# The same kernel with its matmul operands at other SBUF addresses

## The chip, the core and the metric

The kernel runs on one NeuronCore of one Trainium2 chip. The metric is the device time of one execution in microseconds (us); the time before is the median of 3 runs. One execution was also recorded by the hardware profiler; its engines are PE (TensorE matmuls), PEld (TensorE's loads of the stationary operand), DVE (VectorE), ACT (ScalarE), POOL (GpSimd) and SP (which issues most DMAs).

## What is computed

The reference is a network of two blocks on one sequence of 256 tokens with 1024 features, all in float32. The core of it:

```
# first block
h = rms_norm(x);  proj = h @ w_in                      # 1024 x 8352
merged = gate0 * (mla(proj) @ w_br_mla) + gate1 * (dilated(proj) @ w_br_dil) + gate2 * (mem_attention(proj, mem) @ w_br_mem)
x = x + rms_norm(merged @ w_o)
u = rms_norm(x) @ w_ffn_up                             # 1024 x 5632, then a causal convolution of width 3
x = x + rms_norm((silu(gate) * val) @ w_ffn_down)
# second block, two layers
mod = silu(c) @ w_ada + b_ada                          # shift, scale, gate
h = rms_norm(x) * (1 + scale) + shift;  u = h @ w_in_2 # 1024 x 5120
x = x + gate * (concat(rglru(..) * silu(rg_z), mlstm(..) * silu(ml_z)) @ w_out_2)
return rms_norm(x)
```

## The kernel before

Nearly all of the work is matrix products of float32 operands, each written as a sum of two float32r parts. A weight block of 128 partitions and up to 1024 columns comes by DMA into a buffer `raw`; ScalarE casts it to `hi` (L246), VectorE subtracts to get `lo` (L249). Each of `raw`, `hi` and `lo` has four buffers used in turn. The activations are split in the same way: `H` and `L` hold the two parts of the layer's input, eight tiles of 256 tokens in each (8,192 bytes per partition); other pairs, the outputs of attention, the feed-forward's inner activations, the memory's inputs, lie in nine general tiles `s0` to `s8` of the same size ("slots", all shown as `s` in the rows), and the pair of attention outputs in `y`.

Every product is made of three kinds of matmuls (`prod`, L258): activation-high with `hi`, activation-low with `hi`, activation-high with `lo`, four tiles of the contraction at a time. In rows of the trace the name behind the arrow is first the moving operand (the one that streams through the array), then the stationary one (loaded by LDWEIGHTS): `mm<-H,hi` has H moving and the weights stationary, `mm<-hi,s` has the weights moving and a slot stationary. `proj` (features on the partition) streams 256 tokens against 128 weight columns; `proj_long` (token on the partition) streams 512 or 256 weight columns against 128 tokens. There is a load of 128 stationary columns for each matmul, and it runs while the matmul before it streams.

The order of the instructions on each engine is set by the tile framework's scheduler from the program's order and from priorities.

Where a tile lies is set by the order in which the pools are opened, each behind the one before. The lines in question are these:

```
    cp = ctx.enter_context(tc.tile_pool(name="cp", bufs=1))      # constants, xn, H, L
    rawp = ctx.enter_context(tc.tile_pool(name="rawp", bufs=RAW))
    hip = ctx.enter_context(tc.tile_pool(name="hip", bufs=HI))
    lop = ctx.enter_context(tc.tile_pool(name="lop", bufs=LO))
    sp = ctx.enter_context(tc.tile_pool(name="sp", bufs=1))      # slots
...
        hi = hip.tile([P, 1024], F32R, name="hi", tag="hi")
...
        for b in range(0, len(terms), 4):
            for x, y in ((0, 2), (0, 3), (1, 2)):
                for t in terms[b:b + 4]:
                    pe.matmul(dst, lhsT=t[x], rhs=t[y], start=(first and i == 0), stop=(last and i == n - 1))
```

Of the kernel before, what the change touches and what calls it, by code (L numbers as in the profile page):

```python
# [18 lines left out]
P = 128  # L19
S = 256  # L20
# [8 lines left out]
FENCE = 4  # L29
HOLD = 3  # L30
# [77 lines left out]
# products with the token on the partition: output columns in pieces of these widths, as many tiles of rows as make 1024 columns  # L108
# [6 lines left out]
def _long_blocks(kt, pieces=LONG):  # L115
    # for each piece: [(block, tiles)]
    out, n = [], 0
    for w in pieces:
        t = 1024 // w
        out.append([(n + i, range(b, min(kt, b + t))) for i, b in enumerate(range(0, kt, t))])  # L120
        n += len(out[-1])
    return out
# [74 lines left out]
def block_kernel(ctx: ExitStack, tc: tile.TileContext, T: dict, out: bass.AP):  # L197
# [3 lines left out]
    cp = ctx.enter_context(tc.tile_pool(name="cp", bufs=1))  # L201
    rawp = ctx.enter_context(tc.tile_pool(name="rawp", bufs=RAW))
    hip = ctx.enter_context(tc.tile_pool(name="hip", bufs=HI))
    lop = ctx.enter_context(tc.tile_pool(name="lop", bufs=LO))
    sp = ctx.enter_context(tc.tile_pool(name="sp", bufs=1))
# [29 lines left out]
    def hold_loads(*ins):  # L235
        # the next conversions of weights stay behind these instructions of ScalarE and VectorE
        if FENCE:
            fence.update(n=FENCE, ins=[i.ins for i in ins])

    def load(src):  # L240
        n = src.shape[-1]
        raw = rawp.tile([P, 1024], F32, name="raw", tag="raw")[:, :n]
        dma.dma_start(out=raw, in_=src)
        hi = hip.tile([P, 1024], F32R, name="hi", tag="hi")
        with behind(0):
            act.copy(hi[:, :n], raw)  # L246
        lo = lop.tile([P, 1024], F32R, name="lo", tag="lo")
        with behind(1):
            dve.tensor_tensor(out=lo[:, :n], in0=raw, in1=hi[:, :n].bitcast(F32), op=ALU.subtract)  # L249
        fence["n"] -= 1  # L250
        return hi, lo
# [21 lines left out]
    def urgent(on=True):  # L273
        # work at the end of a stage that the tensor engine waits for
        return tc.high_priority(offset=URGENT) if on else nullcontext()

    def proj_long(name, kt, j, H, L, hold=0, beside=(), pieces=LONG):
        # token on the partition, one bank for each block of tokens; the last `hold` weight blocks finish the first tokens early
        w = pieces[j]
        ps = [mm_tile().rearrange("p a b -> p (a b)")[:, :w] for _ in range(2)]  # L280
        blks = _long_blocks(kt, pieces)[j]
        nb = len(blks)
        held = {}

        def part(b, t):
            tb = slice(t * P, (t + 1) * P)
            hi, lo = held[b]
            prod(ps[t], [(H(k)[:, tb], L(k)[:, tb], hi[:, i * w:(i + 1) * w], lo[:, i * w:(i + 1) * w])
                         for i, k in enumerate(blks[b][1])], b == 0, b == nb - 1)

        for b, (n, ks) in enumerate(blks):
            held[b] = load(T[name][n][:, :len(ks) * w])
            if b in beside:
                ada_steps(1)
            if b < nb - hold:
                for t in range(2):
                    part(b, t)
        for t in range(2):
            for b in range(nb - hold, nb):
                part(b, t)  # L300
        return ps

    def proj_first(blks, H, L):
        # tile by tile of the features, one bank for each of the two rows of outputs: starts before all of H is there
        ps = [mm_tile()[:, 0], mm_tile()[:, 0]]
        for k in range(KT):
            hi, lo = (x[:, (k % 4) * 256:(k % 4 + 1) * 256] for x in blks[k // 4])
            for m in range(2):
                mm = slice(m * P, (m + 1) * P)
                prod(ps[m], [(hi[:, mm], lo[:, mm], H(k), L(k))], k == 0, k == KT - 1)  # L310
        return ps
# [17 lines left out]
    ones32 = cp.tile([P, P], F32, name="ones32")  # L329
    dve.memset(ones32, 1.0 / 32.0)  # L330
    eps = cp.tile([P, 1], F32, name="eps")
    dve.memset(eps, EPS)
# [9 lines left out]
    HT = [cp.tile([P, KT, S], F32R, name=n) for n in ("H", "L")]  # L342
# [9 lines left out]
    class Sums:  # L352
        """Sums over the KT tiles of features, token on the partition: one bank for each block of tokens."""
# [5 lines left out]
        def add(self, sq, k):  # L359
            # the first six into the partitions of group k % 4, folded when the last two are still to come  # L360
            if k < 6:
                g = k % 4
                pe.matmul(self.part[32 * g:32 * g + 32], lhsT=ones[:, :32], rhs=sq, start=k < 4, stop=k >= 2)
            if k == 5:
                part = one()
                act.copy(part, self.part)
                self.out = [sm_tile()[:, :P], sm_tile()[:, :P]]
                for t in range(2):
                    pe.matmul(self.out[t], lhsT=part[:, t * P:(t + 1) * P], rhs=ones32, start=True, stop=False)
            if k >= 6:  # L370
                for t in range(2):
                    pe.matmul(self.out[t], lhsT=sq[:, t * P:(t + 1) * P], rhs=ones, start=False, stop=k == 7)
# [9 lines left out]
    def newton(v, n):  # L382
        # 1 / sqrt(v), one Newton step behind the square root
# [8 lines left out]
    def rstd_of(ps, n):  # L392
        # per token, from the sums of squares
# [5 lines left out]
    class Rstd:  # L399
        """1 / sqrt(mean + eps) per token from partial sums of squares, of which the last comes late."""  # L400
# [20 lines left out]
    def root_table(ins):  # L421
        # the square root's table is there before the end of the stage
        with tc.issue_after(ins.ins):
            act.activation(warm, one_c, AF.Sqrt)
# [5 lines left out]
    class Flip:  # L430
        """[token, feature] to [feature, token], four banks of two tiles; a factor per token may go along."""
# [23 lines left out]
    def spread(r):  # L455
        # per-token column to all partitions, token on the free axis
# [50 lines left out]
    def ada_steps(n):  # L507
        # both layers in turn, one step each to finish
# [5 lines left out]
    # =========================== first block ===========================  # L514
    with tc.tile_pool(name="l1", bufs=1) as l1, tc.tile_pool(name="pS", bufs=1) as pS:
# [224 lines left out]
        def dil_proj(p, c, qkv):  # L740
            # queries and keys in turn, then the values
# [65 lines left out]
        # the softmax of a head runs beside the products between its scores and its sums  # L807
# [100 lines left out]
    # the norm's factor is applied to the products of up, before the convolution  # L908
# [36 lines left out]
    # =========================== second block ===========================  # L945
# [10 lines left out]
    def of_head(h, parts):  # L956
        # row 32h on all partitions
# [13 lines left out]
    # half of 8 softplus(-lambda), for both layers  # L971
# [28 lines left out]
    for l in range(2):  # L1000
        # the gate of the layer's output on all partitions, token's side
# [93 lines left out]
        def scores_input(name, h):  # L1095
            # in the place of the memory's input, behind the values
# [56 lines left out]
        em = l2.tile([P, S], F32, name="em", tag="em")  # L1153
# [61 lines left out]
        da = l2.tile([P, S], F32, name="da", tag="da")  # L1215
# [129 lines left out]
```

## Time and profile before

| what | value |
|---|---|
| time, median of 3 runs | 992.81 us (991.2 to 993.47) |
| span of the profiled execution, first to last instruction | 990.5 us |
| what lies between that span and the median | 2.3 us |
| PE busy | 965.9 us (98%), 7,508 matmuls |
| PEld busy | 915.3 us (92%) |
| DVE busy | 736.2 us (74%) |
| ACT busy | 625.1 us (63%) |
| mean granted TensorE clock | 0.994 of full speed |

The profile gives the span of the one execution that it recorded, and no separate time for it; 990.5 us is what the rows of the trace add up to, and the 2.3 us to the median are the start and end of an execution outside them. A matmul's end is modelled in the trace and overlaps the next one's start, so its duration says little; how fast matmuls follow each other is read from their starts.

### The profile page before, as it was taken

The numbers are of one execution on the slowest core, as the hardware profiler recorded it, in microseconds if no ns is written. First come the engines' busy times: TensorE is split into PE (matmuls) and PEld (weight loads), VectorE is DVE, ScalarE is ACT, GpSimd is POOL, SyncE is SP. The second block draws the span as 40 slices with busy tenths as digits, with TensorE's granted clock in tenths as the row PEclk, the third lists the DMA queues.
The fourth block names the chain that finished last, engine by engine and source line by source line (L and its number), as shares of the span: only waits on it lengthen the run. The fifth ranks groups of instructions, "written<-read, shape, count | busy, mean of one in ns | idle before, by whom it ended". The sixth has DMA issues, their size and how long they took to land.

```text
span 990.5 us, 18853 instructions
## 1 busy us (share of the span) xinstructions
PE 965.9 (98%) x7508; PEld 915.3 (92%) x7508; DVE 736.2 (74%) x1267; ACT 625.1 (63%) x1025; POOL 49.9 (5%) x55
## 2 busy tenths in 40 slices
PE   7999999999999999999999999999999999999996
PEld 5999999899989989999979899898989998999986
DVE  5856766667576788888875898588975887687754
ACT  7666555454345478787744786895645876976543
POOL 0000000000000001212200000000002000000021
PEclk9999999999999999999999999999999999999998
DMA  8664575767786746665687365345786355335652
GB/s 295 198 182 136 173 232 193 250 227 225 247 266 211 247 157 206 189 194 190 198 276 244 105 199 168 115 153 194 250 276 200 131 171 170 101 113 193 187 163 75
DMA packets 53225, 190.71 MB, mean 193 GB/s; under 512 B 6064, under 2 KB 6448, under 8 KB 53136
## 3 DMA queue, kind: packets, MB, share of 16 engines
q1 hardware_dynamic: 52128, 185.17, 57.9%
q0 software_dynamic: 1008, 4.33, 1.3%
q8 instruction: 59, 0.97, 0.4%
q14 instruction: 30, 0.25, 0.1%
HBM read 188.42 MB, written 1.05 MB: 191 GB/s over the span
## 4 chain that ended last, share of the span: by engine, by line
PE 71%; DVE 11%; ACT 8%; DMA 6%; issue 4%; POOL 0%; SPq 0%; DVEq 0%; ACTq 0%; POOLq 0%
PE mm L258 59%; DVE lo L249 5%; DMA raw<-in_w_ada 4%; ACT hi L246 3%; ACT fz L934 2%; ACT fw L935 2%; DVE fu L928 1%; PE sm L258 1%; PE sm L1040 1%; DVE raw L494 1%; ACT s L481 1%; PE sm L1196 1%; DMA raw<-in_w_o 1%; PE sm L658 1%; PE sm L1245 1%
## 5 line engine op out<-in xcount | busy, mean ns | idle before, releaser
L249 DVE TENSOR_TENSOR lo<-raw,hi 128x1024 fp32r<-128x1024 f32 (+2 forms) x299 | 372.1, 1255 | 110.4 <-ACT hi L246 108.3
L246 ACT CAST hi<-raw 128x1024 fp32r<-128x1024 f32 (+2 forms) x299 | 308.6, 1042 | 181.2 <-PE mm L258 107.4
L258 PE MATMUL mm<-H,hi 128*128 128x256 f32 x1456 | 238.6, 281 | 0.1
L258 PE MATMUL mm<-L,hi 128*128 128x256 f32 x1456 | 235.8, 279 | 0.1
L258 PE MATMUL mm<-H,lo 128*128 128x256 f32 x1456 | 235.0, 279 | 0.2 <-DVE lo L249 0.2
L258 PEld LDWEIGHTS mm<-H,hi 128*128 128x128 f32 x1456 | 198.9, 188 | 2.2 <-issue 1.6
L258 PEld LDWEIGHTS mm<-L,hi 128*128 128x128 f32 x1456 | 199.0, 188 | 0.4 <-DVE L L1018 0.3
L258 PEld LDWEIGHTS mm<-H,lo 128*128 128x128 f32 x1456 | 198.6, 188 | 0.4 <-DVE lo L249 0.4
L258 PE MATMUL mm<-hi,s 128*128 128x256 f32 (+1 forms) x784 | 149.5, 324 | 0.0
L258 PEld LDWEIGHTS mm<-hi,s 128*128 128x128 f32 x784 | 119.0, 191 | 11.5
L494 DVE CUSTOM_DVE_ANT_0 raw<-raw,c_act 128x1024 f32<-128x1024 f32 x48 | 58.7, 1223 | 55.1 <-DMA raw<-in_w_ada 55.1
L258 PE MATMUL mm<-lo,s 128*128 128x256 f32 (+1 forms) x392 | 85.8, 325 | 2.4 <-DVE lo L249 2.4
L258 PEld LDWEIGHTS mm<-lo,s 128*128 128x128 f32 x392 | 61.7, 192 | 8.8 <-DVE lo L249 3.1
L258 PE MATMUL mm<-s,hi 128*128 128x256 f32 x320 | 56.0, 294 | 0.0
L258 PEld LDWEIGHTS mm<-s,hi 128*128 128x128 f32 x320 | 46.2, 195 | 6.3 <-issue 2.9
L258 PE MATMUL mm<-s,lo 128*128 128x256 f32 x160 | 35.5, 289 | 0.0
L428 ACT ACTIVATE sq<-xn 128x512 f32<-128x512 f32 (+1 forms) x24 | 13.5, 562 | 33.1 <-POOL xn L1309 21.5
L937 POOL TENSOR_TENSOR fz<-fz,fw 128x508 f32<-128x508 f32 x22 | 24.7, 1123 | 130.3 <-DVE fz L936 130.3
L934 ACT ACTIVATE fz<-fu,cols 128x256 f32<-128x256 f32 x44 | 26.1, 594 | 6.5 <-DVE fu L928 6.5
L258 PEld LDWEIGHTS mm<-s,lo 128*128 128x128 f32 x160 | 26.4, 195 | 2.0 <-issue 1.2
L646 ACT ACTIVATE sx<-sx,nm 128x256 f32<-128x256 f32 (+3 forms) x24 | 13.3, 555 | 23.5 <-DVE nm L643 23.5
L481 ACT CAST s<-two 128x512 fp32r<-128x512 f32 x24 | 14.9, 619 | 18.9 <-DVE two L1250 18.9
(315 smaller groups left out, 1146.4 us busy)
## 6 DMA issues: line engine op xcount, KB each, us to landing
raw<-in_w_ada SPq DMA_DIRECT2D x48, 512.0 KB, 4.5
raw<-in_w_up SPq DMA_DIRECT2D x44, 512.0 KB, 4.3
raw<-in_w_out SPq DMA_DIRECT2D x32, 512.0 KB, 4.3
raw<-in_w_down SPq DMA_DIRECT2D x21, 512.0 KB, 4.2
raw<-in_w_mlx SPq DMA_DIRECT2D x16, 512.0 KB, 4.4
raw<-in_w_rgx SPq DMA_DIRECT2D x16, 512.0 KB, 4.2
raw<-in_w_mlo SPq DMA_DIRECT2D x16, 512.0 KB, 4.1
raw<-in_w_rgz SPq DMA_DIRECT2D x16, 512.0 KB, 4.4
```

Of the source, the lines that this page charges most:

```text
L246: act.copy(hi[:, :n], raw)
L249: dve.tensor_tensor(out=lo[:, :n], in0=raw, in1=hi[:, :n].bitcast(F32), op=ALU.subtract)
L258: pe.matmul(dst, lhsT=t[x], rhs=t[y], start=(first and i == 0), stop=(last and i == n - 1))
L428: return act.activation(sq[:, :src.shape[-1]], src, AF.Square, accum_out=acc)
L481: act.copy(hi, src)
L494: dve.tensor_tensor_reduce(out=raw, in0=raw, in1=c_act, op0=ALU.mult, op1=ALU.add, scale=1.0, scalar=0.0, accum_out=mod[:, l, m:m + 1])
L646: act.activation(sx[:, a:b], src, AF.Exp, bias=nm[:, i:i + 1], accum_out=den[:, i:i + 1])
L658: pe.transpose(ps[:, i * P:(i + 1) * P], sx[:, o:o + P], ident)
L928: dve.tensor_tensor(out=u, in0=ps, in1=rs.unsqueeze(1).to_broadcast([P, 2, S]), op=ALU.mult)
L934: act.activation(z[:, i], u[:, i], AF.Identity, scale=col("conv_w", 88 + c), bias=col("conv_b", c))
L935: act.activation(w[:, i], u[:, i], AF.Identity, scale=col("conv_w", c))
L937: pool.tensor_tensor(out=z[:, :, 2:], in0=z[:, :, 2:], in1=w[:, :, :S - 2], op=ALU.add)
```

## The change

The change lays tiles at other addresses. The pool of `H` and `L` now comes first, behind `ones32`, which is widened so that H begins at a multiple of 512 bytes. Then come the pools of `hi` and of `lo`, whose tiles are widened from 1,024 to 1,056 elements (only 1,024 are used), so that each buffer begins 128 bytes further, modulo 512, than the one before. `raw` and the other constants follow, then `eps` as a filler of 32 bytes, then the slots. To make room, the tile `em` takes the buffer of `B`, and `da` that of `R`, in the second block. The comments of the file were taken out too.

```
+STEP = 1056
+FILL_H, FILL_S = 224, 8
...
-    cp = ctx.enter_context(tc.tile_pool(name="cp", bufs=1))
-    rawp = ctx.enter_context(tc.tile_pool(name="rawp", bufs=RAW))
+    hp = ctx.enter_context(tc.tile_pool(name="hp", bufs=1))
+    ones32 = hp.tile([P, FILL_H], F32, name="ones32")[:, :P]
+    dve.memset(ones32, 1.0 / 32.0)
+    HT = [hp.tile([P, KT, S], F32R, name=n) for n in ("H", "L")]
     hip = ctx.enter_context(tc.tile_pool(name="hip", bufs=HI))
     lop = ctx.enter_context(tc.tile_pool(name="lop", bufs=LO))
+    rawp = ctx.enter_context(tc.tile_pool(name="rawp", bufs=RAW))
+    cp = ctx.enter_context(tc.tile_pool(name="cp", bufs=1))
+    fill = ctx.enter_context(tc.tile_pool(name="fill", bufs=1))
+    eps = fill.tile([P, FILL_S], F32, name="eps")[:, 0:1]
+    dve.memset(eps, EPS)
...
-        hi = hip.tile([P, 1024], F32R, name="hi", tag="hi")
+        hi = hip.tile([P, STEP], F32R, name="hi", tag="hi")[:, :1024]
-        lo = lop.tile([P, 1024], F32R, name="lo", tag="lo")
+        lo = lop.tile([P, STEP], F32R, name="lo", tag="lo")[:, :1024]
...
-        em = l2.tile([P, S], F32, name="em", tag="em")
+        em = l2.tile([P, S], F32, name="em", tag="B")
-        da = l2.tile([P, S], F32, name="da", tag="da")
+        da = l2.tile([P, S], F32, name="da", tag="R")
```

The addresses in the two built programs, in bytes from the start of a partition, with the remainder modulo 512 in brackets:

| tile | before | after |
|---|---|---|
| H, L | 33312 (32), 41504 (32) | 17408 (0), 25600 (0) |
| hi, four buffers | 66272, 70368, 74464, 78560 (all 224) | 33792 (0), 38016 (128), 42240 (256), 46464 (384) |
| lo, four buffers | 82656, 86752, 90848, 94944 (all 224) | 50688 (0), 54912 (128), 59136 (256), 63360 (384) |
| raw, four buffers | from 49888 (all 224) | from 67584 (all 0) |
| slots s0 to s8 | from 99040 (all 224) | from 100448 (all 96) |
| y | 196128 (32) | 197536 (416) |

A slice of H, L, a slot or y for one tile of the contraction begins a multiple of 1,024 bytes further on, and one of a weight buffer a multiple of 512, so all slices of a tile have the tile's remainder.

The order of instructions is the same on every engine but for two memsets that VectorE does before anything else. VectorE's first rows before the change (`s_85` and the like are slots; `ones_89` is `ones32`):

```order
L327 MEMSET ones_s 128x256
L330 MEMSET ones_89 128x128
L332 MEMSET eps 128x1
L335 MEMSET one_c 128x1
L477 SCALAR_TENSOR_TENSOR s_112<-s_85,g_mem,s_111 128x256 x2
```

and with it:

```order
L206 MEMSET ones_58 128x128
L214 MEMSET eps 128x1
L337 MEMSET ones_s 128x256
L341 MEMSET one_c 128x1
L482 SCALAR_TENSOR_TENSOR s_118<-s_97,g_mem,s_117 128x256 x2
```

`ones32` and `eps` are set first and `ones_s` behind them; nothing else moved. As an example of the matmuls, a stretch of PE in a product of the first block's gates and the branch product behind it, before (the numbers are those of the tiles):

```order
L258 MATMUL mm_3631<-H_100,hi_3627 128x256 x4
L258 MATMUL mm_3631<-L_101,hi_3627 128x256 x4
L258 MATMUL mm_3631<-H_100,lo_3629 128x256 x4
L258 MATMUL mm_3688<-y_110,hi_3684 128x256 x8
L258 MATMUL mm_3688<-y_110,lo_3686 128x256 x4
```

and with the change, where all numbers are other but the sequence is the same:

```order
L268 MATMUL mm_3637<-H_60,hi_3633 128x256 x4
L268 MATMUL mm_3637<-L_61,hi_3633 128x256 x4
L268 MATMUL mm_3637<-H_60,lo_3635 128x256 x4
L268 MATMUL mm_3694<-y_116,hi_3690 128x256 x8
L268 MATMUL mm_3694<-y_116,lo_3692 128x256 x4
```

Nothing moved there but the lines of the source.

## Rows read from the trace of the kernel before

**Rows 1.** The page: busy time of each engine, granted clock in 40 slices.

```profile
PE 965.9 (98%) x7508; PEld 915.3 (92%) x7508; DVE 736.2 (74%) x1267; ACT 625.1 (63%) x1025; POOL 49.9 (5%) x55
...
PEclk9999999999999999999999999999999999999998
```

**Rows 2.** The page: chain of work that ended last, shares of the span.

```profile
PE 71%; DVE 11%; ACT 8%; DMA 6%; issue 4%; POOL 0%; SPq 0%; DVEq 0%; ACTq 0%; POOLq 0%
```

**Rows 3.** Waits over the whole span: us in total, times, longest.

```profile
DVE lo L249 <- ACT hi L246: 108.3, 113, 4.0
ACT hi L246 <- PE mm L258: 107.4, 100, 3.5
```

**Rows 4.** Groups of matmuls by shape: busy us, mean ns | idle before.

```profile
L258 PE MATMUL mm<-H,hi 128*128 128x256 f32 x1456 | 238.6, 281 | 0.1
...
L258 PE MATMUL mm<-hi,s 128*128 128x512 f32 x288 | 79.6, 395 | 0.0
L258 PE MATMUL mm<-hi,s 128*128 128x256 f32 x496 | 70.6, 283 | 0.0
L258 PE MATMUL mm<-s,hi 128*128 128x256 f32 x320 | 56.0, 294 | 0.0
L258 PE MATMUL mm<-lo,s 128*128 128x512 f32 x144 | 45.6, 397 | 2.4 <-DVE lo L249 2.4
L258 PE MATMUL mm<-lo,s 128*128 128x256 f32 x248 | 40.2, 283 | 0.0
L258 PE MATMUL mm<-s,lo 128*128 128x256 f32 x160 | 35.5, 289 | 0.0
```

**Rows 5.** Timeline of PE, 38 to 73 us: start, us, instruction, count.

```profile
38.42 0.64 PE L258 MATMUL mm<-H,hi 128*128 128x256 f32 x4
...
72.34 0.83 PE L379 MATMUL sm<-ones_s,s 128*128 128x128 f32 x6
```

**Rows 6.** Timeline of PE in the feed-forward's first product, 424 to 478 us.

```profile
424.02 0.62 PE L258 MATMUL mm<-L,hi 128*128 128x256 f32 x4
...
477.51 0.62 PE L258 MATMUL mm<-H,lo 128*128 128x256 f32 x4
```

**Rows 7.** Timeline of PE, 534 to 549 us: weights moving, slots stationary, 256 columns.

```profile
534.12 0.64 PE L258 MATMUL mm<-lo,s 128*128 128x256 f32 x4
...
549.24 0.40 PE L258 MATMUL mm<-hi,s 128*128 128x256 f32 x2
```

**Rows 8.** Timeline of PE: 512 weight columns moving against H and L.

```profile
280.04 0.63 PE L258 MATMUL mm<-hi,L 128*128 128x512 f32 x2
...
282.84 0.63 PE L258 MATMUL mm<-hi,L 128*128 128x512 f32 x2
```

**Rows 9.** Timeline of PE: 512 weight columns moving against slots.

```profile
952.09 0.61 PE L258 MATMUL mm<-lo,s 128*128 128x512 f32 x2
...
958.89 0.61 PE L258 MATMUL mm<-lo,s 128*128 128x512 f32 x2
```

**Rows 10.** Timeline of PE, 315.8 us: float32 matmuls of 128 columns.

```profile
315.83 0.83 PE L783 MATMUL sm<-pt,s 128*128 128x128 f32 x6
316.50 1.50 PE L785 MATMUL sm<-pt,s 128*128 128x128 f32 x12
```

**Rows 11.** Window 380 to 478 us: PE, PEld, DVE, ACT, POOL busy, PEclk, DMA share, GB/s.

```profile
380.00:478.00 98.00, 98.00 (x867) 98.00 (x867) 87.47 (x125) 79.82 (x143) 18.84 (x18) 1.00 0.61 192
```

**Rows 12.** Groups of VectorE by shape: the weights' subtraction, and one half as wide.

```profile
L249 DVE TENSOR_TENSOR lo<-raw,hi 128x1024 fp32r<-128x1024 f32 x293 | 366.9, 1263 | 106.6 <-ACT hi L246 104.5 <-PE mm L258 1.3
...
L482 DVE TENSOR_TENSOR s<-two,s 128x512 fp32r<-128x512 f32 x24 | 16.4, 684 | 4.3 <-ACT s L481 4.1
```

**Rows 13.** Timeline at the start: VectorE's memset of `ones32`, PE's first matmul.

```profile
1.18 0.17 DVE L330 MEMSET ones<- 128x128 f32 x1
...
6.99 1.06 PE L363 MATMUL sm<-sq,ones_s 128*32 128x256 f32 x2 [6.99 <-DVE s L477]
```

More of the change, by code (lines that the diff above doesn't have):

```diff
@@ L328, in block_kernel @@
     ones = ones_s[:, :P]
[L329 to L332, printed above, removed]
     c_act = cp.tile([P, D], F32, name="c_act")
@@ L340, in block_kernel @@
     half = cp.tile([P, 56], F32, name="half")
-    HT = [cp.tile([P, KT, S], F32R, name=n) for n in ("H", "L")]
     H, L = kth(HT[0]), kth(HT[1])
```

## The prediction

> **What bounds the kernel now.** [...] The chain that ended last goes through PE for 71% of the span; the rest is mostly VectorE, ScalarE and DMA, the making of weight blocks [rows 2]. The waits tell how these hang together: VectorE's `lo` waits for ScalarE's `hi` (108.3 us in all), and `hi` waits for matmuls (107.4 us), that is for a buffer that TensorE gives back [rows 3]. The loads are held up by TensorE, not the other way round: what makes matmuls follow each other faster moves nearly everything behind them.
>
> So the distance from one matmul's start to the next is the number to read, by kind of operands. [...]
>
> - H or L moving (address 32 modulo 512), weights stationary (224): from 38.42 to 72.34 us there are 288 matmuls without a break, 33.92 us / 288 = 117.8 ns [rows 5].
> - The same operands at the same addresses in the product of up: 424.02 to 477.51 us, 118 groups of four, 53.49 / 472 = 113.3 ns [rows 6].
> - Weights moving, slots stationary (both 224): 534.12 to 549.24 us, 126 matmuls, 15.12 / 126 = 120.0 ns [rows 7].
> [...]
>
> [...] And one pair of addresses has two steady distances, 117.8 and 113.3; each holds for tens of microseconds. [...]
>
> **The change, part by part.** No instruction is added, and no product, wait or DMA is moved. Three small things first. The two memsets that come earlier are VectorE's, 0.17 us for `ones32`, 5.8 us ahead of TensorE's first matmul, which waits for later things [rows 13]: nothing, and if that cover were gone, 0.2 us. `em` in the buffer of `B` waits for the last reader of `B`, a VectorE addition from whose result `em` is made anyway, and `da` in that of `R` comes after the readers of `R` by a whole stage: nothing. Operands of VectorE and ScalarE move too. The subtraction takes 1,263 ns for 1,024 columns, and one of 512 takes 684 [rows 12], so 579 ns for the second half, 1.13 ns a column, with all three operands at one remainder; I take no change. Were it a tenth dearer, it would be hidden, since VectorE is busy for 736 us of the span [rows 1]; only in the product of up, where it is busy for 87.47 of 98 us [rows 11], would the window's 18 products with 2 subtractions each (36 x 0.126 = 4.5 us) come near the edge.
>
> What remains is TensorE's distance. Modulo 512, moving less stationary was 320 for H and L, and 0 for slots. With the change it depends on the buffer: 0, 384, 256, 128 for H and L, one after the other as the buffers come round; 96, 480, 352, 224 for slots that move, and the opposite of these for slots that stand still. Of these the trace shows only 0, and only with both at 224. So the price has to be bounded. The lower end for 256 columns is 111.7 ns: float32 matmuls with an ordinary load of 128 columns each start 0.67 us / 6 apart [rows 10], the shortest that rows show beside such a load. [...]
>
> Counts [rows 4]: 3 x 1,456 = 4,368 matmuls with H or L moving. Some 1,050 of them are the product of up at 113.3 (22 products of 48; 867 lie in the window of rows 11, 98 us); for the other 3,318 I take 117.8. With slots and 256 columns 496 + 248 + 320 + 160 = 1,224, at 120.0; with 512 columns 288 + 144 = 432, at 226.7.
>
> My choice between the ends: I take it that runs whose loads come from another remainder with each block do not keep to the dearer of two steady states, and 113.3 is a state that these very matmuls hold through all of up. So H and L go to 113.3: 3,318 x 4.5 ns = 14.9 us. Slots leave the distance 0, which is the dearest seen at 256 columns; I take the 117.8 that is next to it: 1,224 x 2.2 = 2.7 us. The 512-column ones I leave where they are. Sum 17.6 us. Of this, between 71% (TensorE's share of the chain) and 97.5% (its busy share) arrives at the end, 12.5 to 17.2 us; I take 90%, 15.8 us, since the loads wait for TensorE. The profiled span goes from 990.5 to 974.7, and with the 2.3 us between span and median the time goes from 992.8 to **977.0 us**.
>
> **The rivals.**
>
> *Nothing changes.* [...] For it: the same addresses give 113.3 and 117.8 [rows 5, 6]. Against it: no stretch of slots reads as H and L do [rows 7], and 512 columns are dearer against H and L than against slots [rows 8, 9]. Time: 992.8, give or take the 4.7 us that up would lose if it fell into the other state (1,050 x 4.5 ns). Chance 0.10. [...]
>
> *Slower: multiples of 128 are as bad as 0.* Distance 0 gave 120.0 ns without exception [rows 7], and H at 0 against the first of the four buffers at 0 is a distance of 0. If what matters repeats every 128 bytes, all of H's and L's matmuls go to 120.0, and up loses its 113.3: 3,318 x 2.2 + 1,050 x 6.7 = 7.3 + 7.0 = 14.3 us, 1,007 us. The point from which it decides is the mean of H and L now, (3,318 x 117.8 + 1,050 x 113.3) / 4,368 = 116.7 ns: above that after the change, the kernel is slower. For it: that buffer, and that 113.3 was reached with an odd multiple of 64. Against it: nothing shows a period of 128. Chance 0.27, milder cases included; at the upper end of the price, 126.7 ns, it would be 29.5 + 14.1 + 8.2 = 52 us (1,045), which I hold for unlikely.
>
> *Half of it.* The buffer at 0 costs 120.0, the other three give 113.3, mean 115.0: 4,368 x 1.7 = 7.4 us, with the slots' 2.7 and the 90% 9.1 us: 983.7. Chance 0.15.
>
> *More than forecast.* [...] Chance 0.13.
>
> **How the numbers follow.** The forecast has 0.35. Faster by over 0.2% (about what a measurement of this kernel can tell from no change) are the forecast, half and more: 0.63. The same is the first rival: 0.10. Slower: 0.27. For eight in ten I leave out the lowest part of the last rival and the upper half of the slower one: 957 to 1,004 us. Within the forecast alone the range is 968 to 982: slots at 120.0 and the share of 71% (14.9 x 0.71 = 10.6 us) to slots at 111.7 and 97.5% ((14.9 + 10.2) x 0.975 = 24.5 us).
>
> **What would show it.** In the profile after, PE's timeline: 33.92 us for the 288 matmuls of rows 5 become 32.6 if H and L go to 113.3, and up keeps its 113.3. Were they apart by buffer, groups of four with `hi` and `lo` of one block would read otherwise than those of the next. Slots: 126 matmuls in 14.8 us, not 15.12. Waits of `hi` for matmuls [rows 3] shrink, and PE's busy share stays near 97%. The prediction is wrong if up is slower than 113.3, if slots go above 120.0, or if PE becomes faster and then waits for `lo`, which would say that the loads are the bound.

## The result, and the profile after

The changed kernel is slower: 997.51 us median of 4 runs (996.38 to 998.86), against 992.53 us of the kernel before on the same chip (991.2 to 993.47, 4 runs). The ratio is 1.0054, with a 95% interval of 1.0039 to 1.0068. The prediction said 977.0 us. The profiled execution has a span of 996.1 us, 5.6 more than before.

The page of the kernel after: busy time of each engine, granted clock in 40 slices, and the chain that ended last. They answer to [rows 1] and [rows 2].

```profile
PE 974.3 (98%) x7508; PEld 922.0 (93%) x7508; DVE 728.0 (73%) x1267; ACT 628.1 (63%) x1025; POOL 50.1 (5%) x55
...
PEclk9999999999999999999999999999999999999999
...
PE 90%; DMA 4%; DVE 3%; ACT 2%; issue 1%; SPq 0%; DVEq 0%; ACTq 0%
```

TensorE is busy for 8.4 us more with the same 7,508 instructions, at a mean granted clock of 0.996 (0.994 before), and it stands in 90% of the chain, where it stood in 71%. So the matmuls follow each other more slowly. Its timeline in the kernel after shows where: first H and L moving, then slots against 256 columns, then slots against 512 columns.

```profile
38.13 0.64 PE L268 MATMUL mm<-H,hi 128*128 128x256 f32 x4
...
72.37 2.39 PE L384 MATMUL sm<-ones_s,s 128*128 128x128 f32 x20
...
522.58 0.63 PE L268 MATMUL mm<-lo,s 128*128 128x256 f32 x4
...
532.49 0.63 PE L268 MATMUL mm<-lo,s 128*128 128x256 f32 x4
...
956.30 0.63 PE L268 MATMUL mm<-lo,s 128*128 128x512 f32 x2
...
963.31 0.63 PE L268 MATMUL mm<-lo,s 128*128 128x512 f32 x2
```

The 288 matmuls of [rows 5] take 34.24 us, 118.9 ns each, where 117.8 stood before and 113.3 was forecast. The slots of [rows 7] improve: 84 matmuls in 9.91 us, 118.0 ns instead of 120.0. The 512 columns of [rows 9], which the prediction left alone, get dearer: 30 in 7.01 us, 233.7 ns instead of 226.7. The product of up is next, in windows of the kernel after (all its matmuls between its first full block and the first of the next product, w_down; then w_down's 130 matmuls of 512 columns). The columns are those of [rows 11].

```profile
369.21:491.30 122.09, 122.09 (x1029) 122.09 (x1028) 95.23 (x149) 99.44 (x172) 22.94 (x21) 1.00 0.59 190
491.30:521.63 30.33, 30.33 (x132) 24.42 (x131) 23.60 (x53) 15.78 (x24) 3.56 (x4) 1.00 0.78 257
```

The same two windows in the kernel before:

```profile
367.01:483.41 116.40, 116.40 (x1030) 116.40 (x1028) 102.46 (x147) 95.29 (x169) 21.72 (x20) 1.00 0.62 194
483.41:517.35 33.94, 31.57 (x132) 25.39 (x131) 26.22 (x56) 18.37 (x28) 4.64 (x5) 0.95 0.76 253
```

Up holds 1,027 matmuls between these two starts, so its distance went from 113.3 to 118.9 ns, and that cost 5.7 us. The next window gives 3.6 us back, although its 512 columns are dearer: TensorE has no gap in it any more (30.33 of 30.33 us busy, 31.57 of 33.94 before) and its granted clock reads 1.00 (before 0.95). What stood there before is this: two rows of TensorE's timeline in the kernel before, and a window of the same kernel just behind them (us, PE busy, granted clock, DMA share, GB/s):

```profile
506.23 1.09 PE L258 MATMUL mm<-hi,s 128*128 128x512 f32 x4
509.70 0.73 PE L258 MATMUL mm<-lo,s 128*128 128x512 f32 x2 [2.37 <-DVE lo L249]
```

```profile
510.00:514.60 4.60, 4.60 (x14) 0.63 0.88 295
```

A 2.37 us wait for VectorE's `lo`, and behind it 4.6 us in which the granted clock reads 0.63 in the mean, 0.50 from 511.1 to 514.5 us. The page's row of 40 slices [rows 1] shows a 9 there. The starts of the windows give the account of the span: the kernel after is 2.2 us late at up (369.21 against 367.01), 7.9 late at w_down (491.30 against 483.41), 4.3 late at its 256 columns (521.63 against 517.35), and 5.6 at the end.

The waits of the loads, in the kernel after, answer to [rows 3]. Both grew, where the prediction had the second shrinking: a buffer comes free later when TensorE is slower.

```profile
DVE lo L259 <- ACT hi L256: 126.8, 116, 4.1
ACT hi L256 <- PE mm L268: 121.4, 122, 3.5
```

### The profile page after: what moved, and what is told of

Its sections match the earlier page's. It is cut to its first block, busy times and chain, and to the rows that moved or that the text cites. A ratio compares the mean times of both kernels' runs of the same rounds, so it can differ in the third digit from the quotient of the medians.

```text
span 996.1 us, 18853 instructions
## 1 busy us (share of the span) xinstructions
PE 974.3 (98%) x7508; PEld 922.0 (93%) x7508; DVE 728.0 (73%) x1267; ACT 628.1 (63%) x1025; POOL 50.1 (5%) x55
## 4 chain that ended last, share of the span: by engine, by line
PE 90%; DMA 4%; DVE 3%; ACT 2%; issue 1%; SPq 0%; DVEq 0%; ACTq 0%
PE mm L268 78%; DMA raw<-in_w_ada 2%; PE sm L268 1%; PE sm L1045 1%; DVE lo L259 1%; DMA raw<-in_w_dv 1%; PE sm L663 1%; PE sm L1201 1%; PE sm L1250 1%; PE sm L790 1%; PE sm L1241 0%; PE sm L724 0%; PE sm L451 0%; DVE raw L499 0%; DMA s<-in_memT 0%
## 5 line engine op out<-in xcount | busy, mean ns | idle before, releaser
L259 DVE TENSOR_TENSOR lo<-raw,hi 128x1024 fp32r<-128x1024 f32 (+2 forms) x299 | 363.8, 1226 | 128.2 <-ACT hi L256 126.8
L256 ACT CAST hi<-raw 128x1024 fp32r<-128x1024 f32 (+2 forms) x299 | 309.3, 1044 | 201.6 <-PE mm L268 121.4
L268 PE MATMUL mm<-H,hi 128*128 128x256 f32 x1456 | 241.3, 284 | 0.1
L268 PE MATMUL mm<-H,lo 128*128 128x256 f32 x1456 | 240.2, 283 | 0.0
L268 PE MATMUL mm<-L,hi 128*128 128x256 f32 x1456 | 238.9, 282 | 0.1
L268 PEld LDWEIGHTS mm<-L,hi 128*128 128x128 f32 x1456 | 202.8, 189 | 0.4 <-DVE L L1023 0.3
L268 PEld LDWEIGHTS mm<-H,lo 128*128 128x128 f32 x1456 | 202.9, 190 | 0.0
L268 PEld LDWEIGHTS mm<-hi,s 128*128 128x128 f32 x784 | 117.4, 189 | 12.9
L486 ACT CAST s<-two 128x512 fp32r<-128x512 f32 x24 | 14.9, 620 | 19.2 <-DVE two L1255 19.2
L268 PE MATMUL mm<-y,hi 128*128 128x256 f32 x192 | 26.7, 281 | 0.0
```

The costliest lines, as they stand in the source:

```text
L486: act.copy(hi, src)
```

## The experiments

**The theories.** The word distance has two meanings here: with ns, the time from one matmul's start to the next; without, the difference of addresses in bytes, moving less next stationary, modulo 512 where nothing else is said. *D*: what counts is the distance between the moving operand and the next stationary one, modulo some power of two. *A*: each operand's own alignment counts. *S*: the remainder that changes from buffer to buffer is what costs. Later ones are stated with the runs.

The table gathers all runs. The distances in ns are means over matmuls that follow each other without a gap; for each matmul the time to the next start was taken from the trace, and its operands' addresses from the program. "Up" is the product of up, "H, L" all others with H or L moving. The times are medians, the ratios to the kernel before on the same chip. The distances come from one profiled execution of each kernel, and it need not be a typical one: e1's was the slowest of ten (994.40 us), e8's the fastest of six (985.83; the slowest took 991.68). In which state runs of matmuls stood in the other executions is not recorded.

```
kernel                 H, L   up     weights  slots on  512 on  us      ratio (95%)
                                     on slots weights   slots
before                 117.7  113.3  119.9    119.6     227.5   992.53
after                  118.9  118.9  118.1    119.2     233.4   997.51  1.0054 (1.0039-1.0068)
e1 old distances       117.4  117.8  119.9    119.5     227.4   991.67  0.9995 (0.9983-1.0007)
e2 H at 64             114.6  113.5  118.1    119.1     233.2   983.48  0.9909 (0.9894-0.9924)
e3 no step             119.8  120.0  118.4    119.6     234.1   1002.18 1.0102 (1.0083-1.0121)
e4 distance 32         116.8  116.7  120.0    119.5     227.3   989.79  0.9973 (0.9959-0.9987)
e5 all at 64           114.4  113.5  116.1    115.3     230.9   978.98  0.9868 (0.9839-0.9896)
e6 64, no step         114.5  113.3  117.6    114.3     229.2   981.48  0.9887 (0.9858-0.9916)
e7 64, step 256        115.2  113.4  115.8    117.6     233.3   984.09  0.9910 (0.9885-0.9936)
e8 64, other half      117.6  113.3  114.4    115.0     229.0   987.97  0.9963 (0.9940-0.9986)
e9 hi and lo apart     114.0  113.3  117.8    116.9     230.0   978.95  0.9861 (0.9841-0.9880)
e10 the same and step  114.1  113.4  117.2    115.4     230.6   979.68  0.9862 (0.9839-0.9885)
```

**e1, the old distances in the new layout.** All pools stand in the new order, but the operands are as far apart modulo 512 as before (H and L 0, all weights and slots 192).

```diff
-STEP = 1056
-FILL_H, FILL_S = 224, 8
+STEP = 1024
+FILL_H, FILL_S = 224, 112
     HT = [hp.tile([P, KT, S], F32R, name=n) for n in ("H", "L")]
+    dve.memset(hp.tile([P, 48], F32, name="pad_h"), 0.0)
```

> The changed layout, but with every distance (moving less stationary, modulo 512) as it was before: H and L at 0, all weight buffers at 192, slots at 192, y at 0. Theory D (the distance decides): H and L against weights go back from 118.9 to 117.8 ns with the product of up at 113.3 or 117.8, slots at 256 columns from 118.4 to 120.0, 512 columns against slots from 233 to 226.7; the time to 992.5 us, or 997 if up falls into its other state. Theory A (each operand's own alignment decides, H at a multiple of 512 being dear): H and L stay at 118.9, 997 us or more. Theory S (the remainder that changes from one weight buffer to the next is what costs): as D, since there is no step.

The timeline of TensorE in this run has the same 288 matmuls in 33.92 us, to the hundredth as before.

```profile
37.73 0.64 PE L269 MATMUL mm<-H,hi 128*128 128x256 f32 x4
...
71.65 2.40 PE L385 MATMUL sm<-ones_s,s 128*128 128x128 f32 x20
```

With other alignments for every operand, the distances and the time (0.9995) are those of before: D holds, A falls, and the rest of the change (order of pools, early memsets, shared buffers) costs nothing outside the interval, which ends at 1.0007. Up fell into its other state here, 117.8 ns, which makes it 4.6 us longer (120.95 against 116.40). Of that, w_down's first window gave back 2.0 (31.90 against 33.94) and a few runs of H and L that started at 113.3 gave 0.8; the profiled span is 2.2 us longer than before, a difference that the medians don't show.

**e2, H and L moved by 64 bytes.** All else is as in the change: weights at 0, 128, 256, 384 and slots at 96.

```diff
-FILL_H, FILL_S = 224, 8
+FILL_H, FILL_S = 240, 8
     HT = [hp.tile([P, KT, S], F32R, name=n) for n in ("H", "L")]
+    dve.memset(hp.tile([P, 112], F32, name="pad_h"), 0.0)
```

> The changed kernel with H and L at 64 modulo 512 instead of 0; the weight buffers keep their steps of 128 (0, 128, 256, 384), slots stay at 96. The distances of H and L are then 64, 448, 320, 192 in turn, all 64 away from a multiple of 128, as before the change. Theory D with a period of 128 or 256: H and L at 117.8 ns in spite of the steps (3,318 x 1.1 = 3.6 us less than the changed kernel), and up at 113.3 if it finds that state again (5.9 us less): 988 to 994 us. Theory S: 118.9 everywhere, 997.5 us. Theory A: no forecast for 64; 997.5 if 64 is as dear as 0.

The timeline of the 288 matmuls again:

```profile
38.93 0.64 PE L269 MATMUL mm<-H,hi 128*128 128x256 f32 x4
39.40 0.63 PE L269 MATMUL mm<-L,hi 128*128 128x256 f32 x4
39.87 0.63 PE L269 MATMUL mm<-H,lo 128*128 128x256 f32 x4
40.34 0.62 PE L269 MATMUL mm<-H,hi 128*128 128x256 f32 x4
40.79 0.62 PE L269 MATMUL mm<-L,hi 128*128 128x256 f32 x4
...
71.62 2.39 PE L385 MATMUL sm<-ones_s,s 128*128 128x128 f32 x20
```

The first three groups of four start 0.47 us apart, the following 0.45: the run enters at 117.8 ns, drops when the buffer changes, and stays there (288 in 32.69 us, 113.5 ns). Not every run drops at its first change of buffer; of that more under e9. The time is 983.48 us, 14.0 less than with the change, for 64 bytes of one pair of operands. S falls: a step between buffers is no cost in itself.

**e3, no step.** Only `STEP = 1024` instead of 1056, so that all weights are at 0, as H and L.

> The changed kernel without the step: all weight buffers at 0 modulo 512, H and L at 0, slots at 96. Distances are then 0 for H and L throughout, 96 for slots that move, 416 for slots that stand. Theory D: H and L at the 120.0 ns that slots at distance 0 had before, 4,368 x 1.1 = 4.8 us more than the changed kernel, 1,002 us; 512 columns stay near 233 ns. Theory S: without the step H and L fall back to 117.8 or less, 994 us or less.

```profile
37.64 0.63 PE L268 MATMUL mm<-H,hi 128*128 128x256 f32 x4
...
72.18 2.40 PE L384 MATMUL sm<-ones_s,s 128*128 128x128 f32 x20
```

That timeline gives 34.54 us / 288 = 119.9 ns. Distance 0 is as dear for H and L as for slots. The 120.0 ns that the rival "multiples of 128 are as bad as 0" had put on all of H and L come true only here, with every buffer at 0, at 1,002 us.

**e4, distance 32 in the old layout.** Eight floats behind H and L in the kernel before bring the distance from 320 to 288; slots stay at 0.

```diff
     HT = [cp.tile([P, KT, S], F32R, name=n) for n in ("H", "L")]
+    dve.memset(cp.tile([P, 8], F32, name="pad_h"), 0.0)
```

> The kernel before with one pad of 32 bytes between L and the weights, which shifts everything behind it by 32: H and L stay at 32, weights, slots at 256. Only the distance of H and L changes, from 320 to 288 (32 modulo 256); slots stay at distance 0 and y at 320. Theory D: in the changed kernel, matmuls at distances 32 and 288 followed each other every 116.7 ns, so H and L go to 116.7 everywhere: 3,318 x 1.1 = 3.6 us less, and up, which had 113.3, 3.6 us more: 992.5 us, no change in the sum, with up at 116.7. Theory A: H has not moved, so up keeps 113.3 and the others 117.8 unless the weights' own alignment (a multiple of 256 instead of 224) counts.

H and L go to 116.8 and up to 116.7, about the figure that `y` shows at 32 and 288 in the kernel after (116.7 to 116.8). That is faster than before (0.9973), although up is 3.4 us longer (119.82 against 116.40); why that costs nothing is told below. The gain lies ahead of up, which starts 2.8 us earlier than before (364.24 against 367.01): 1,374 matmuls with H or L moving take 0.9 ns less each, and from 360.9 to 364.3 us the granted clock reads 1.00 here and 0.50 in the kernel before.

**e5, every pair at an odd multiple of 64.** As the change, with H and L at 0, weights at 64, 192, 320, 448, slots at 256 and y at 128.

```diff
-FILL_H, FILL_S = 224, 8
+FILL_H, FILL_S = 224, 32
     HT = [hp.tile([P, KT, S], F32R, name=n) for n in ("H", "L")]
+    dve.memset(hp.tile([P, 16], F32, name="pad_h"), 0.0)
...
+        dve.memset(l1.tile([P, 16], F32, name="pad_y"), 0.0)
         yT = l1.tile([P, 8, S], F32R, name="y", tag="y")
```

> Every pair of operands an odd multiple of 64 bytes apart (H and L at 0, weight buffers at 64, 192, 320 and 448, slots at 256, y at 128 modulo 512), buffers 128 bytes apart modulo 512 as in the change. Theory K (at such a distance matmuls of 256 columns have two steady pitches, 117.8 and 113.3 ns, and a change of the distance by 128 pushes a run into the shorter): H and L as with H at 64 (114.5 outside up, 113.4 in up), and slots and y now too, from 118.6 to about 114.5 in 1,224 matmuls, 5.0 us; 512 columns half at 228.8 and half at 233, 1 us less; of these 6 us nine tenths arrive: 978 us against 983.5 with H at 64 alone. Rival (the runs of slots are too short, or too mixed, to be pushed): slots stay at 117.8, 982 us. If the making of weight blocks has become the bound by now, pitches fall but the time stays at 983 and the waits of PE for lo grow.

Measured 978.98 us, as K said; slots improve less evenly. The timeline of weights against slots has 12 matmuls from row to row:

```profile
518.06 0.63 PE L269 MATMUL mm<-lo,s 128*128 128x256 f32 x4
...
519.47 0.62 PE L269 MATMUL mm<-lo,s 128*128 128x256 f32 x4
...
520.83 0.62 PE L269 MATMUL mm<-lo,s 128*128 128x256 f32 x4
...
522.20 0.63 PE L269 MATMUL mm<-lo,s 128*128 128x256 f32 x4
...
523.60 0.62 PE L269 MATMUL mm<-lo,s 128*128 128x256 f32 x4
```

1.41, 1.36, 1.37 and 1.40 us: in this direction the runs drop and climb again with the buffers (117.8 and 117.4 at 64 and 320, 113.8 and 115.4 at 192 and 448), while H and L, once at 113.3, stay.

**e6, the same without the step**: e5 with `STEP = 1024`, so all weights at 64.

> The same, but all four weight buffers at 64 modulo 512, so that the distance stays one and the same within a run. Theory K: runs stay in the state in which they began, mostly 117.8, now and then 113.3; H and L 117.5, slots and y 117.8 instead of 119.5 to 120.0 at distance 0, 512 columns near 229: 989 to 990 us. Rival F (an odd multiple of 64 is enough, and the old layout met 117.8 for another reason): H and L at 113 to 114.5, 978 us, as with the step.

```profile
38.34 0.63 PE L269 MATMUL mm<-H,hi 128*128 128x256 f32 x4
...
71.00 2.39 PE L385 MATMUL sm<-ones_s,s 128*128 128x128 f32 x20
...
536.03 0.63 PE L269 MATMUL mm<-lo,s 128*128 128x256 f32 x4
...
538.86 0.63 PE L269 MATMUL mm<-lo,s 128*128 128x256 f32 x4
```

K fails here: 288 matmuls in 32.66 us (113.4 ns) and 114.5 over all H and L, without any change of remainder, 981.48 us. But rival F, which fits H and L, doesn't fit slots: 24 matmuls in 2.83 us, 117.9 ns. H and L stand at 448 (192 modulo 256), where e1 and before had 320 (64 modulo 256).

**e7, buffers 256 bytes apart**: H and L at 128, weights at 192, 448, 192, 448, slots at 256, y at 64.

```diff
-STEP = 1056
-FILL_H, FILL_S = 224, 8
+STEP = 1088
+FILL_H, FILL_S = 128, 1
     HT = [hp.tile([P, KT, S], F32R, name=n) for n in ("H", "L")]
+    dve.memset(hp.tile([P, 16], F32, name="pad_h"), 0.0)
...
-    one_c = cp.tile([P, 1], F32, name="one_c")
-    dve.memset(one_c, 1.0)
+    one_c = ones_s[:, 0:1]
```

> The same again, but the four weight buffers 256 bytes apart modulo 512 (192, 448, 192, 448), H and L at 128, slots at 256, y at 64. The distance changes from block to block, but only by 256. If what matters repeats every 256 bytes, as the pitches by distance in the kernel after say (equal at 0 and 256, at 128 and 384, at 96 and 352), this is no change, and runs stay where they began: 989 to 991 us, H and L at 117.5. Rival (any change of remainder pushes a run): 978 to 980 us, H and L at 114.5.

H and L read 115.2 ns and 984.09 us came out, between K's range and the rival's. Run by run there are only two values, 117.8 and 113.3, and past its first block no run of H and L goes from one to the other: a step of 256 is no step, as K said. Of its 54 runs of H and L 35 settle in the shorter state in their first block, far more than K allowed; that goes with the distance, 192 modulo 256, as in e6, where 42 of 54 do.

**e8, the other half**: e6 with 48 floats behind H and L instead of 16, so that H and L stand at 320 to the weights, and not at 448.

> All four weight buffers at 192 modulo 512, H and L at 0, slots at 384, y at 256: one distance per pair of operands as in the run without a step, but each in the other half of 256 bytes (H and L against weights 320, that is 64 modulo 256, where it was 448, that is 192; slots against weights 192, weights against slots 320, so these two stay in their halves; y 64). Theory B (at odd multiples of 64 there are two steady pitches; a run takes one in its first matmuls and holds it; 192 modulo 256 takes 113.3 mostly, 64 takes 117.8 mostly): H and L go from 114.5 to 117.5 and up from 113.3 perhaps to 117.8, 10 to 15 us, so 991 to 996 us. Rival P (which state a run takes hangs on what runs ahead of it, and not on the half): H and L stay near 114.5, 981 us.

```profile
37.00 0.63 PE L269 MATMUL mm<-H,hi 128*128 128x256 f32 x4
...
70.92 2.39 PE L385 MATMUL sm<-ones_s,s 128*128 128x128 f32 x20
...
533.24 0.62 PE L269 MATMUL mm<-lo,s 128*128 128x256 f32 x4
...
535.96 0.62 PE L269 MATMUL mm<-lo,s 128*128 128x256 f32 x4
```

For H and L, B holds and P falls: the 288 matmuls are back at 33.92 us, and the mean at 117.6. 51 of the 54 runs of H and L settle at 117.8. The time, 987.97 us, is 6.5 above e6, less than expected: in the profiled execution up stayed at 113.3, and weights on slots improved by 3 ns. The slots are what B can't explain: weights on slots at 320 hold 113.3 ns (24 in 2.72 us) where the same distance held 117.9 in e6. So the half of the 256 bytes is not all that picks the state.

**e9, hi and lo 128 bytes apart**: e6 with 32 floats between the pools of `hi` and `lo`; the distance changes inside each block. Slots and `y`, which lie behind, move by 128 bytes with `lo`.

```diff
     hip = ctx.enter_context(tc.tile_pool(name="hip", bufs=HI))
+    mid = ctx.enter_context(tc.tile_pool(name="mid", bufs=1))
+    dve.memset(mid.tile([P, 32], F32, name="pad_m"), 0.0)
     lop = ctx.enter_context(tc.tile_pool(name="lop", bufs=LO))
```

> All hi buffers at 64, all lo buffers at 192, H and L at 0, slots at 384, y at 256: the distance changes by 128 inside each block, from the products of hi to those of lo, and not from buffer to buffer. If a change by 128 pushes a run of H and L into 113.3 and a change back doesn't lift it, every run of H and L reaches 113.3 within its first 12 matmuls: 113.5 everywhere, against 114.35 with the step from buffer to buffer, 3 to 4 us off 979: 975 us. Rival (the push needs a change of buffer, or lasts only as long as the distance 192): H and L between 113.3 and 117.8, 115 to 116, 983 us.

One run of H and L in its timeline, a group of four to a row:

```profile
908.11 0.63 PE L271 MATMUL mm<-H,hi 128*128 128x256 f32 x4
908.58 0.64 PE L271 MATMUL mm<-L,hi 128*128 128x256 f32 x4
909.05 0.63 PE L271 MATMUL mm<-H,lo 128*128 128x256 f32 x4
909.52 0.63 PE L271 MATMUL mm<-H,hi 128*128 128x256 f32 x4
909.99 0.62 PE L271 MATMUL mm<-L,hi 128*128 128x256 f32 x4
910.44 0.62 PE L271 MATMUL mm<-H,lo 128*128 128x256 f32 x4
910.90 0.62 PE L271 MATMUL mm<-H,hi 128*128 128x256 f32 x4
```

0.47 us to a group up to the one behind the first `lo`, then 0.45 to 0.46: every run of H and L is at 113.3 within two blocks, and the mean is 114.0. The push doesn't need a change of buffer, and the change back doesn't lift H and L. The direction matters: the distance goes from 192 modulo 256 (`hi`) to 64 (`lo`) at 909.05 and back to 192 at 909.52, and the starts draw together only behind the second change. Counted over the matmuls' starts in e2, e5, e9 and e10, runs of H and L at 117.8 dropped at 122 of 141 changes from 64 to 192 and at 4 of 83 from 192 to 64; none at 113.3 rose at either, in 1,332. The expected 975 us were missed by 4: H and L stopped at 114.0, not 113.5 (3,318 x 0.5 = 1.7 us), and the slots went the wrong way (117.8 and 116.9 instead of e5's 116.1 and 115.3, some 2 us). **e10** adds the step between buffers to this (`STEP = 1056`):

> Both: buffers 128 bytes apart and hi 128 bytes from the lo of the same block (hi at 64, 192, 320, 448; lo at 192, 320, 448, 64). If each push helps, as the one before or a little better, 974 to 977 us. If a push from hi to lo in one direction is a lift in the other, as the pitches of weights against slots by block say (117.8 at 64 and 320, 113.4 to 115 at 192 and 448), H and L stay at 114 to 115 and the time at 979 to 981 us.

Its 979.68 us can't be told from e5 and e9. These three are the best versions found, 1.3% to 1.4% faster than the kernel before.

## Why the prediction was wrong

**What bounds the kernel.** Right nearly everywhere: the loads wait for TensorE (`hi` for 121.4 us in the kernel after, where PE is busy for 98% of the span), and the distance between matmuls sets the time. Wrong in one place, of which [rows 4] had a sign, 2.4 us of waiting for `lo`. Behind up at 113.3 ns, w_down's first 130 matmuls wait for their loads: 33.94 us before. All kernels with up at 113.3 to 113.5 have 33.7 to 34.7 us there, except e8 with 32.4 (the clock reads 1.00 in it, 0.95 in the others); those with up at 116.7 to 120.0 have 30.1 to 30.5, and e1 31.9. So e4 loses nothing by its slower up: up and this window together take 149.92 us in e4, 150.34 before. Up's distance isn't the whole reason, though. With up at 117.8, e1 still waits there, first row, and e4 with 116.7 hardly does, second row:

```profile
514.65 0.74 PE L269 MATMUL mm<-lo,s 128*128 128x512 f32 x2 [2.06 <-DVE lo L260]
508.12 0.73 PE L258 MATMUL mm<-lo,s 128*128 128x512 f32 x2 [0.26 <-DVE lo L249]
```

Nor does such a wait always bring the lower clock: e1 and e8, with 2.06 and 2.39 us of it, keep 1.00 in this window. What else decides on the wait and the clock there stays open.

**The small things and the other engines, at nothing: right**, by e1.

**"H and L go to 113.3": the step that failed.** The choice was that runs whose remainder changes with each block don't keep to the dearer of two steady states. The runs showed that it depends on the distance whether there is a cheaper state at all. At multiples of 128 none of the runs took 113.3: in the kernel after, 119.3 ns at 0, 118.6 at 128, 119.2 at 256, 118.7 at 384. So the 3,318 went from 117.7 to 118.9 (+4.0 us), not to 113.3 (-14.9), and up lost its 113.3 (+5.7), which the prediction had named as a sign of being wrong. Only at odd multiples of 64 do both states, 117.8 and 113.3, appear; there, the rule that the prediction took does hold in the main, for changes from 64 to 192 (e2, e5, e9). It was read from a distance of 320 and applied to 0, 128, 256 and 384.

**The rival that came true** is the slower one. Its deciding point, 116.7 ns, was passed with 118.9. Its mechanism (what matters repeats, and 128 is like 0) is right in kind: the values repeat every 256, and 128 is 0.7 ns better than 0. Its price of 120.0 was therefore too high, and it counted no giving back: 1,007 against 997.5 us.

**Slots at 117.8: right direction, sized too large.** Weights on slots reach 118.1 (744 x 1.8 = 1.3 us), slots on weights 119.2 (480 x 0.4 = 0.2 us): 1.5 us and not 2.7.

**"The 512-column ones I leave where they are": failed.** 0 is the cheapest distance at 512 columns (227.5 ns before), though with 96 the dearest at 256. With the slots at 96 all four buffers read 233 to 234 ns: 432 x 5.9 = 2.5 us lost. [rows 8] against [rows 9] had said as much: 12 matmuls in 2.80 us, 233.3 ns, at a distance of 192, against 30 in 6.80 us, 226.7 ns, at 0.

**The share of 90%: failed.** 4.0 + 5.7 + 2.5 - 1.5 = 10.7 us at TensorE became 5.6 at the end. Most of the difference is the 3.6 us (4.4 with the dearer columns: 130 x 5.9 ns = 0.8 us) that w_down's window gave back.

**The ends of the price.** No run shows the 126.7 ns that the prediction names as its upper end: the dearest means at 256 columns were 120.0 ns (up in e3, weights on slots in e4). Nor does a run show what the 957 us at the lower end of the range would take: the shortest means were 113.3 ns at 256 columns and 227.3 at 512 (e4), and the fastest kernel took 978.95 us (e9).

**"Nothing changes": ruled out.** e2 against the change moves H and L by 64 bytes and nothing else that TensorE reads in these products (modulo 512), and takes up from 118.9 to 113.5 ns a matmul at a granted clock of 1.00.

**What stays open**: what picks the state in which a run begins at odd multiples of 64. H and L start more often at 113.3 at 192 modulo 256 (42 of 54 runs in e6, 35 in e7) and nearly always at 117.8 at 64 (51 of 54 before and in e8), but up held 113.3 at 320 in before and in e8 and 117.8 in e1, and weights on slots held both at 320. No kernel here varies alone what runs ahead of a run. Nor is it told apart whether the stationary operand that counts is the next one or the one in use: within a block both have the same remainder. Why the distance between matmuls goes with the addresses, no run shows.

## What to carry to other kernels

Read the distance from one matmul's start to the next for each kind of operands, and sort it by the difference of their addresses modulo 256 before anything is laid out: a good value at one difference says nothing of another (up took 113.3 ns a matmul at 320 before, 118.9 with the change). Here the moving and the stationary operand should differ by an odd multiple of 64 bytes (192 modulo 256, or changing from 64 to 192 within a run: 114.0 to 115.2 ns over H and L in e2, e5 to e7, e9 and e10, against 117.7 before), and 512-column operands want differences of 0 or 64 (227 to 231 ns, against 230 to 234 at the others). Before a faster stage is counted as gain, look at the window behind it: the next stage may wait for its buffers there, and part of the gain is lost again (here w_down's window moved by 3.6 us against the 5.7 of up).

## What the runs showed of the hardware

- At 256 float32r columns against a 128-column load, the distance between matmuls goes with the address difference (moving less next stationary) modulo 256: 0 gives 119.2 to 120.0 ns, 32 gives 116.7 to 117.1 (three runs of H and L in e4 hold 117.8), 96 119.6 to 120.0, 128 118.5 to 118.9, 160 117.6 to 119.3, 224 118.2 to 118.4. At 64 and 192 runs of H and L hold either 117.8 or 113.3; weights on slots in e9, whose distance changes every few matmuls, read 118.8 at 64. Only multiples of 32 were tried. Where the granted clock reads 0.50, H and L against weights follow each other every 213 ns (before, 362.63 to 364.12 us).
- At 512 columns: 227 to 231 at 0, 229 to 231 at 64, 230 to 234 at all others.
- The two states at 64 and 192 last: a run of 1,027 matmuls keeps the one that it has reached, across changes of buffer. A change of the difference from 64 to 192 mostly moves a run of H and L from 117.8 to 113.3 (122 of 141), one from 192 to 64 hardly ever (4 of 83), and none moves it back; one by 256 does nothing (e7).
- VectorE's subtraction of 1,024 columns went from 1,263 ns [rows 12] to 1,233 with the change. The addresses are not the reason, since those that run beside no work of GpSimd take 1,221 ns before and 1,222 after. Beside GpSimd's TENSOR_TENSOR in up one takes up to 1.73 us. Before, with up at 113.3 ns, nearly every second subtraction there meets it (20 of 44; first two rows); in the kernel after, with up at 118.9, it mostly comes behind it (4 of 45 meet it; last two rows):

```profile
423.55 1.09 POOL L937 TENSOR_TENSOR fz<-fz,fw 128x508 f32<-128x508 f32 x1 [4.45 <-DVE fz L936]
424.00 1.72 DVE L249 TENSOR_TENSOR lo<-raw,hi 128x1024 fp32r<-128x1024 f32 x1 [0.62 <-ACT hi L246]
```

```profile
443.91 1.09 POOL L942 TENSOR_TENSOR fz<-fz,fw 128x508 f32<-128x508 f32 x1 [4.61 <-DVE fz L941]
445.03 1.23 DVE L259 TENSOR_TENSOR lo<-raw,hi 128x1024 fp32r<-128x1024 f32 x1 [1.29 <-ACT hi L256]
```

  All kernels with up at 113.3 to 113.5 read 1,261 to 1,263 ns, all others 1,232 to 1,238.
